# A two-layer decoder trunk: pairs' weights in their own buffer on GpSimd's queue, two gate halves split by transfers, and turned blocks placed first on ScalarE

## The chip, the cores and the metric

The kernel runs on one core of one Trainium2 chip. The time is the device time of one execution in microseconds (us); lower is better. A profiled execution is taken by the hardware profiler and shows, for each engine, when each instruction ran and what ended the idle time before it.

Engines, by the names of the profile: PE is TensorE's products, PEld its weight loads, DVE is VectorE, ACT is ScalarE, POOL is GpSimd, SP is SyncE, which here issues nearly all transfers. A DMA "lands" when its data is there and its semaphore says so. L12 is line 12 of the kernel before.

## What is computed

A trunk of two pre-norm residual layers over 256 tokens of width 1024, all in float32. Cut to what matters here:

```python
for i in range(2):
    u = rmsnorm(h, attn_norm_g[i])
    h = h + mixer_i(u) @ w_o[i]             # 16 heads of 64; layer 0 forgetting attention, layer 1 MoBA
    u = rmsnorm(h, ffn_norm_g[i])
    gu = u @ ffn_w_in[i]                    # 1024 x 5632
    h = h + (silu(gu[:, :2816]) * gu[:, 2816:]) @ ffn_w_out[i]     # 2816 x 1024
    gate = sigmoid(rmsnorm(h, ple_norm_g[i]) @ ple_w_gate[i])      # 1024 x 1024
    h = h + gate * (p[i] @ ple_w_up[i])     # p: 256 x 256
return rmsnorm(h, final_norm_g)
```

## The kernel before, in words

**Products of halves.** float32 operands are split into a rounded high half (type fp32r) and the low rest, `lo = x - hi`. A product is three products of halves: high by high, high by low, low by high (`mm3`, L94 to L98). So every block of weights is loaded by SyncE into a raw tile, rounded into `whi` by ScalarE and subtracted into `wlo` by VectorE: `half` (L129, the splits at L158 and L159), `blocks`, and `gapped` (L167, splits at L175 and L176), whose weights are padded to 1080 columns. `raw` has six buffers, `whi` and `wlo` six each. A `raw` buffer is free when VectorE has made the low half; a `whi` slot is free when TensorE has used it.

**Order.** The program is written once, in one order; a scheduler then fixes each engine's order, and each engine executes strictly in that order, waiting on semaphores. `tc.issue_after(ins)` puts the instructions written inside it behind `ins` on the engine of `ins`; it adds no wait between engines. `tc.keep_in_program_order` fixes the order of the products at the end.

**Norms.** `Norm` (L181) turns h by TensorE transposes (`turn`, L196, result in PSUM tile `tp`). For each of the eight blocks of 128 columns ScalarE writes the high half times the norm's gain (`g`, L192) and VectorE the low half (L193). `square` (L206) lets ScalarE sum squares, `root` (L213) makes the factor 1/rms with one GpSimd power (`col`, L220), which is applied later.

**Before the FFN.** At the end of `attention` h is finished, squared and scaled (`hn`), with GpSimd's powers `coln` (L581, L582). `ple_up` (L754) makes p @ ple_w_up: four PSUM banks (`pu`), each copied by ScalarE into `ut` (L763; the trace names the tile uh). Then `nf.turn` transposes hn and the eight turned blocks are made.

**The FFN** (`ffn`, L590). There are 22 column tiles f of 128. `up([f])` makes gate and up products (`gu`, 48 products of 256 columns per f); `up([0, 1])` does two tiles together. `gated` (L647) applies silu and the product into `a`. Two tiles f make a unit u, eleven units in all. A unit's down projection runs as a scheme of seven block products instead of eight (`product`, L628, tile `fo`): it needs sums of activation blocks (L665 to L667, then split into `ah` and `al` by `halves`, L671) and sums of weight blocks. `unit(u)` (L599) loads the unit's weights of ffn_w_out in two transfers of 512 KB into `ru` (L603, raw buffers), splits them (`p0`, `p3`), makes four sums in `xs` (L617, L619, L622; two buffers, `xs2[:, u % 2]`) and splits these (`p1`, `p2`; L596 ScalarE into `uh`, L597 VectorE into `ul`). From f = 4 on, `visit` puts 11 of the 21 products of a unit ahead of the even f and 10 ahead of the odd f, so that a unit's period is 21 products of 512 columns and 96 of 256 columns. The second product of high halves by `al` is the third of its visit. The last unit's split halves take `whi` and `wlo` slots.

**The gate.** After the last visits `gate` takes the first two halves of ple_w_gate with `half()`. `onto` adds the sums to h, `np_.turn(0)` transposes the first four blocks, `np_.square(0)` squares, and two more halves follow. `ple` (L765) makes the products `pg` (`pair_unit`, one half for two blocks k), in the middle `nm.turn(1)`, `nm.square(1)` and `nm.root()`.

Of the kernel before, what the change touches and what calls it, by code (L numbers as in the profile page):

```python
# [46 lines left out]
HW = 1024  # L47
HC = 512
NCHUNK = 54
WARM = 10  # L50
RAW = 6
# [3 lines left out]
LINE = 64  # L55
# [13 lines left out]
NU = FT // 2  # L69
# [6 lines left out]
def trunk(ctx: ExitStack, tc: tile.TileContext, x, xg, wx, xr, pt, w, wu, cst, gf, rel, hot, rvm, out):  # L76
    nc = tc.nc
# [49 lines left out]
    state = {"next": 0}  # L127

    def half(at=0, entry=0):  # L129


        i = state["next"]
        state["next"] += 1
        if i not in (1, 2):
            raw = work.tile([P, HW + LINE], F32, tag="raw", bufs=RAW, name=f"raw{i}")
        ht, lt = (work.tile([P, HW + 2 * LINE], F32R, tag=n, bufs=6, name=f"{n}{i}") for n in ("whi", "wlo"))
        hi, lo = ht[:, at:at + HW], lt[:, at:at + HW]
        if entry:
            nc.sync.dma_start(raw[:, 0:HW], w[i - 2][:, 0:HW])
            nc.scalar.activation(hi, raw[:, 0:HW], AF.Copy)  # L140
            ats = [(at + FURTHER, 0, entry), (at + LINE, entry, HW)]
            for a, c0, c1 in ats:
                nc.vector.tensor_tensor(lt[:, a + c0:a + c1], raw[:, c0:c1], f32(hi[:, c0:c1]), op=ALU.subtract)
            return hi, [lt[:, a + k * P:a + (k + 1) * P] for a, c0, c1 in ats for k in range(c0 // P, c1 // P)]
        if i in (1, 2):
            raw = hw[:, i - 1, S:]
        parts = 2 if i < 2 else 1
        for q in range(parts):
            c = slice(q * HW // parts, (q + 1) * HW // parts)
            if i in (1, 2):  # L150
                at = slice(c.start + (S if q else 0), c.stop + S)
                nc.sync.dma_start(hw[:, i - 1, at], wx[i - 1][:, at])
            else:
                nc.sync.dma_start(raw[:, c], w[max(i - 2, 0)][:, c])
            if i + q == 0:
                nc.vector.tensor_copy(hi[:, c], raw[:, c])
            else:
                nc.scalar.activation(hi[:, c], raw[:, c], AF.Copy)  # L158
            nc.vector.tensor_tensor(lo[:, c], raw[:, c], f32(hi[:, c]), op=ALU.subtract)  # L159
        return hi, lo  # L160
# [17 lines left out]
        return [[t[:, c:c + P] for c in cs] for t in (ht, lt)]  # L178


    class Norm:  # L181


# [5 lines left out]

        def block(self, m, src):  # L190
            g = gn[:, self.n, m:m + 1]
            nc.scalar.activation(self.hi[:, m], src, AF.Copy, scale=g)  # L192
            self.last = nc.vector.scalar_tensor_tensor(self.lo[:, m], src, g, f32(self.hi[:, m]),  # L193
                                                       op0=ALU.mult, op1=ALU.subtract)

        def turn(self, hf, src=h, keep=lambda i: i):  # L196

            for b in (2 * hf, 2 * hf + 1):
                tp = bank(f"tp{self.n}_{b}")
                for n in range(4):  # L200
                    m, t = 2 * b + n // 2, n % 2
                    keep(nc.tensor.transpose(tp[:, n * P:(n + 1) * P], src[:, t, m * P:(m + 1) * P], ident))
                for n in range(2):
                    self.block(2 * b + n, tp[:, n * S:(n + 1) * S])

        def square(self, hf):  # L206
            for t in range(2):
# [28 lines left out]
    nm = Norm(0)  # L236
# [31 lines left out]
    def tokens(o, x, t, w, start, stop):  # L268

        at = slice(t * P, (t + 1) * P)  # L270
        mm3(o, (x[0][:, at], x[1][:, at]), w, start, stop)
# [109 lines left out]
    def attention(layer, nm, mid, early, nf, fill):  # L381
# [191 lines left out]
        for t in range(2):  # L573
# [8 lines left out]
            nc.gpsimd.tensor_tensor(r, r, nhalf[:, 0:1], op=ALU.pow)  # L582
            nc.scalar.activation(hn[:, t, 0:HC], h[:, t, 0:HC], AF.Copy, scale=r)
            nc.vector.tensor_scalar(hn[:, t, HC:D], h[:, t, HC:D], r, None, op0=ALU.mult)
        ple_up(layer, pp, ut)
        for hf in range(2):
            nf.turn(hf, hn)
        return ut

    def ffn(layer, nm):  # L590
        xs2 = work.tile([P, 2, 4, HC], F32, tag="act", name=f"xs{layer}")
        np_ = Norm(3 * layer + 2)
        left, right = {}, {}

        def splits(hi, lo, src):
            nc.scalar.activation(hi, src, AF.Copy)  # L596
            return nc.vector.tensor_tensor(lo, src, f32(hi), op=ALU.subtract)  # L597

        def unit(u):  # L599

            r1, r2 = (work.tile([P, HW + LINE], F32, tag="raw", bufs=RAW, name=f"ru{layer}_{u}_{i}") for i in range(2))
            for i, r in enumerate((r1, r2)):
                nc.sync.dma_start(r[:, 0:HW], wu[layer * NU + u][:, i * HW:(i + 1) * HW])  # L603
            xs = xs2[:, u % 2]

            def pair(n, wide=HW):
                if u == NU - 1:
                    return [work.tile([P, HW + 2 * LINE], F32R, tag=t, bufs=6, name=f"{t}u{layer}_{n}")[:, 0:wide]
                            for t in ("whi", "wlo")]
                return [stage.tile([P, wide], F32R, tag=f"{t}{n}", bufs=1, name=f"{t}{n}_{layer}_{u}")  # L610
                        for t in ("uh", "ul")]

            p0 = pair(0)
            splits(*p0, r1[:, 0:HW])
            p3 = pair(3, HC)
            splits(*p3, r2[:, HC:HW])
            nc.vector.tensor_tensor(xs[:, 0:2], r2[:, 0:HC].unsqueeze(1).to_broadcast([P, 2, HC]),  # L617
                                    r1[:, 0:HW].rearrange("p (a c) -> p a c", c=HC), op=ALU.add)
            nc.vector.tensor_tensor(xs[:, 2], xs[:, 0], r1[:, HC:HW], op=ALU.add)  # L619
            p1 = pair(1)  # L620
            splits(*p1, xs[:, 0:2].rearrange("p a c -> p (a c)"))
            nc.vector.tensor_tensor(xs[:, 3], xs[:, 2], r2[:, HC:HW], op=ALU.add)  # L622
            p2 = pair(2)
            splits(*p2, xs[:, 2:4].rearrange("p a c -> p (a c)"))
            cut = lambda p, i: [t[:, i * HC:(i + 1) * HC] for t in p]
            right[u] = {1: cut(p0, 0), 3: cut(p0, 1), 2: p3, 5: cut(p1, 0), 7: cut(p1, 1), 6: cut(p2, 0), 4: cut(p2, 1)}
# [52 lines left out]
        def up(fs):  # L679

            bks = {f: bank(f"gu{layer}_{f}") for f in fs}

            def step(f, a, wt, k, start):
                mm3(bks[f][:, a * S:(a + 1) * S], (wt[0][k], wt[1][k]), nm.k(k), start, k == KT - 1)

            if fs[0] == 0:
                wts = {f: (blocks() if f else gapped(), blocks()) for f in fs}
                for k in range(KT):
                    for f in fs:
                        for a in range(2):  # L690
                            step(f, a, wts[f][a], k, k == 0 and a == 0)
            else:
                for a in range(2):
                    wt = blocks() if a else gapped()
                    for k in range(KT):
                        step(fs[0], a, wt, k, k == 0)
            for f in fs:
                gated(f, bks[f])

        up([0, 1])  # L700
        up([2])
        up([3])
        acc = {i: bank(f"fo{layer}_{i}") for i in (1, 3, 2, 5, 7, 6, 4)}
        for f in range(4, FT):
# [1 line left out]
            up([f])  # L706
        for u in (NU - 2, NU - 1):
            unit(u)
        gate = [half(), half()]
        def last(u, *which):  # L710
            for i in which:
                for n in range(3):
# [5 lines left out]

        last(NU - 2, 1, 2, 6, 7, 4)
        last(NU - 1, 1, 2, 6, 7, 4)  # L720
        with tc.issue_after(left["end"].ins):
            onto(0, 0, acc[1])
            onto(0, 0, acc[2])
        u2 = work.tile([P, HC], F32, tag="t2k", bufs=3, name=f"u2_{layer}")
# [9 lines left out]
        np_.turn(0, h, tc.keep_in_program_order)  # L734
        with tc.issue_after(got.ins):
            onto(0, 1, u2, ALU.subtract)
        with tc.issue_after(np_.last.ins):
            onto(1, 1, u3, ALU.subtract)
            onto(1, 1, acc[5])
            onto(0, 1, acc[5])  # L740
            got = onto(0, 1, acc[3])
        np_.square(0)
        with tc.issue_after(got.ins):
            gate += [half(), half()]
        return np_, gate

    def ple_in(layer):
# [6 lines left out]
    def ple_up(layer, pp, ut):  # L754
        phi, plo = pp
        wt = [half(), half()]
        for hf in range(2):
            cols = slice(hf * HC, (hf + 1) * HC)
            for t in range(2):
                bk = bank(f"pu{layer}_{hf}_{t}")  # L760
                for k in range(2):
                    tokens(bk, (phi[:, k], plo[:, k]), t, [w[:, cols] for w in wt[k]], k == 0, k == 1)
                nc.scalar.activation(ut[:, t, cols], bk, AF.Copy)  # L763

    def ple(layer, nm, ut, nx, early):  # L765

# [9 lines left out]
        for c in range(4):  # L776
            pair_unit(bks[0], c, early[c], nm.k, mid=(lambda: nm.turn(1)) if c == 1 else None)
            if c == 1:
                nm.square(1)
                nm.root()  # L780
                table(AF.Sigmoid, nm.col[:, 0:1])
        for t in range(2):
# [194 lines left out]
```

## Time and profile before

| | |
|---|---|
| runs, median (lowest to highest) | 657.89 us (656.99 to 659.89), three runs |
| profiled execution, its own time | 657.68 us |
| its span | 655.8 us |
| TensorE busy | 637.9 us (97%) |
| VectorE busy | 525.7 us (80%) |
| ScalarE busy | 422.7 us (64%) |
| GpSimd busy | 14.8 us (2%), 27 instructions |
| granted TensorE clock, mean | 0.997 |
| DMA, mean rate over the span | 191 GB/s |

The span is the time between the first and the last event of the program on the core; the execution's own time is 1.9 us longer. A row of the timeline has the start in us from the start of the span, the duration, the engine, the line, the instruction, the tile written and the tiles read, their shapes, the count, and in brackets the idle time before it and what ended that. Products are pipelined: TensorE starts the next one before the modelled end of the one before, so that the distance of two starts, not the duration, is the price of a product. A wait in the lists is "engine line waited for: us in total, times, longest us".

### The profile page before, as it was taken

How to read it: one execution, taken by the hardware profiler on the slowest of the kernel's cores; microseconds unless marked ns; L12 is line 12 of the kernel's file. 1: busy time of each engine (PE TensorE's matmuls, PEld its weight loads, DVE VectorE, ACT ScalarE, POOL GpSimd, SP SyncE). 2: the span in 40 equal slices, each digit the busy share in tenths (PEclk: the TensorE clock that was granted, in tenths of full speed). 3: DMA queues.
4: the chain of work that ended last, by engine and by line, in shares of the span. 5: the costliest groups of instructions: out<-in, count | busy, mean ns of one | idle time of the engine just before them, and what ended most of it. 6: DMA issues, size and time to landing. Idle time of an engine off the chain costs nothing.

```text
span 655.8 us, 11673 instructions
## 1 busy us (share of the span) xinstructions
PE 637.9 (97%) x4514; PEld 575.6 (88%) x4514; DVE 525.7 (80%) x828; ACT 422.7 (64%) x725; POOL 14.8 (2%) x27
## 2 busy tenths in 40 slices
PE   9999999999999999999999999999999999999995
PEld 7899987899989899997889999789999888989874
DVE  5878874799888888898875787659888888889985
ACT  6966674777655566557666677667766555555663
POOL 1000000100000000000200000010000000000001
PEclk9999999999999999999999999999999999999998
DMA  8969544467656666541797554444675665655501
GB/s 336 385 223 313 173 129 147 147 196 263 196 198 196 195 198 196 194 146 51 245 356 222 180 170 132 132 130 152 222 235 179 196 195 194 199 195 171 183 1 64
DMA packets 36022, 125.20 MB, mean 191 GB/s; under 512 B 3904, under 2 KB 6272, under 8 KB 35968
## 3 DMA queue, kind: packets, MB, share of 16 engines
q1 hardware_dynamic: 35552, 124.07, 57.6%
q8 instruction: 35, 0.57, 0.4%
q10 hardware_dynamic: 416, 0.40, 0.2%
q14 instruction: 19, 0.16, 0.1%
HBM read 123.39 MB, written 4.22 MB: 195 GB/s over the span
## 4 chain that ended last, share of the span: by engine, by line
PE 62%; DVE 16%; DMA 10%; issue 6%; ACT 4%; POOL 1%; POOLq 0%; DVEq 0%; ACTq 0%
DMA ru<-wu 9%; PE fo L632 7%; PE gu L97 6%; PE gu L98 6%; PE gu L96 6%; DVE wlo L176 5%; PE pq L96 5%; PE pq L97 4%; PE pq L98 4%; DVE wlo L159 4%; PE wo L96 2%; PE v L97 2%; PE v L98 2%; PE wo L97 2%; PE wo L98 2%
## 5 line engine op out<-in xcount | busy, mean ns | idle before, releaser
L96 PE MATMUL gu<-g,whi 128*128 128x256 f32 x704 | 194.0, 277 | 1.9 <-ACT g L192 1.9
L97 PE MATMUL gu<-g,whi 128*128 128x256 f32 x704 | 194.6, 277 | 0.5 <-DVE g L193 0.5
L98 PE MATMUL gu<-g,wlo 128*128 128x256 f32 x704 | 194.5, 277 | 0.0
L158 ACT ACTIVATE whi<-raw 128x1024 fp32r<-128x1024 f32 (+1 forms) x122 | 128.3, 1057 | 94.9 <-PE gu L97 51.4
L159 DVE TENSOR_TENSOR wlo<-raw,whi 128x1024 fp32r<-128x1024 f32 (+1 forms) x123 | 147.7, 1211 | 28.0 <-ACT whi L158 27.8
L96 PEld LDWEIGHTS gu<-g,whi 128*128 128x128 f32 x704 | 131.8, 188 | 3.8 <-ACT g L192 2.3
L97 PEld LDWEIGHTS gu<-g,whi 128*128 128x128 f32 x704 | 132.2, 188 | 2.4 <-DVE g L193 0.9
L98 PEld LDWEIGHTS gu<-g,wlo 128*128 128x128 f32 x704 | 132.1, 188 | 0.0
L175 ACT ACTIVATE whi<-raw 128x1080 fp32r<-128x1080 f32 x47 | 52.2, 1112 | 57.9 <-PE gu L97 40.2
L176 DVE TENSOR_TENSOR wlo<-raw,whi 128x1080 fp32r<-128x1080 f32 x47 | 60.0, 1277 | 18.4 <-ACT whi L175 18.3
L96 PE MATMUL pq<-g,whi 128*128 128x256 f32 x256 | 71.5, 279 | 0.0
L97 PE MATMUL pq<-g,whi 128*128 128x256 f32 x256 | 70.9, 277 | 0.0
L98 PE MATMUL pq<-g,wlo 128*128 128x256 f32 x256 | 70.9, 277 | 0.0
L632 PE MATMUL fo<-uh,al 128*128 128x512 f32 x140 | 56.3, 402 | 4.9 <-DVE al L597 4.8
L617 DVE TENSOR_TENSOR xs<-ru,ru 128x1024 f32<-128x1024 f32 x22 | 26.9, 1223 | 38.0 <-DMA ru<-wu 38.0
L632 PE MATMUL fo<-uh,ah 128*128 128x512 f32 x140 | 55.0, 393 | 0.0
L632 PE MATMUL fo<-ul,ah 128*128 128x512 f32 x140 | 54.8, 392 | 0.0
L96 PEld LDWEIGHTS pq<-g,whi 128*128 128x128 f32 x256 | 48.2, 188 | 1.1 <-issue 0.6
L597 DVE TENSOR_TENSOR ul<-xs,uh 128x1024 fp32r<-128x1024 f32 x40 | 48.7, 1217 | 0.0
L97 PEld LDWEIGHTS pq<-g,whi 128*128 128x128 f32 x256 | 48.1, 188 | 0.0
L98 PEld LDWEIGHTS pq<-g,wlo 128*128 128x128 f32 x256 | 48.1, 188 | 0.0
L596 ACT ACTIVATE uh<-xs 128x1024 fp32r<-128x1024 f32 x40 | 40.3, 1057 | 6.3 <-DVE xs L617 5.6
(189 smaller groups left out, 1129.6 us busy)
## 6 DMA issues: line engine op xcount, KB each, us to landing
raw<-w SPq DMA_DIRECT2D x122, 512.0 KB, 4.5
raw<-w SPq DMA_DIRECT2D x47, 540.0 KB, 4.5
ru<-wu SPq DMA_DIRECT2D x44, 512.0 KB, 4.0
d<-d SPq DMA_DIRECT2D x4, 768.0 KB, 9.8
bias<-d SPq DMA_DIRECT2D x4, 512.0 KB, 5.2
h<-x SPq DMA_DIRECT2D x2, 512.0 KB, 9.2
hw<-wx SPq DMA_DIRECT2D x1, 640.0 KB, 6.4
hw<-xr SPq DMA_DIRECT2D x1, 640.0 KB, 8.3
```

The lines of the kernel that those rows point to most:

```text
L96: mm(o, ah, bh, start=start, stop=False, skip_group_check=True)
L97: mm(o, ah, bl, start=False, stop=False, skip_group_check=True)
L98: mm(o, al, bh, start=False, stop=stop, skip_group_check=True)
L158: nc.scalar.activation(hi[:, c], raw[:, c], AF.Copy)
L159: nc.vector.tensor_tensor(lo[:, c], raw[:, c], f32(hi[:, c]), op=ALU.subtract)
L175: nc.scalar.activation(ht, raw[:, 0:WW], AF.Copy)
L176: nc.vector.tensor_tensor(lt, raw[:, 0:WW], f32(ht), op=ALU.subtract)
L596: nc.scalar.activation(hi, src, AF.Copy)
L597: return nc.vector.tensor_tensor(lo, src, f32(hi), op=ALU.subtract)
L617: nc.vector.tensor_tensor(xs[:, 0:2], r2[:, 0:HC].unsqueeze(1).to_broadcast([P, 2, HC]), r1[:, 0:HW].rearrange("p (a c) -> p a c", c=HC), ...
L632: got = mm(acc[i], a[x][:, SLOT[i]], b[y], start=u == 0 and n == 0, stop=u == NU - 1 and n == 2, skip_group_check=True)
```

## The change

It has three parts.

*Pairs' weights.* The "act" buffer that held two sets of sums now holds one set (`xs`) and the two halves of a unit's raw weights (`ru1`, `ru2`). Units 0 to 9 load these through GpSimd's queue; the last unit still uses two raw buffers and SyncE. The halves `p3` get a second buffer and leave the `whi` and `wlo` slots in the last unit.

*First gate halves.* `summed()` takes the place of `half()` for the first two halves of ple_w_gate: a transfer on GpSimd's queue writes the weight into hi, of type fp32r, and so rounds it; ScalarE writes -hi into lo; a second transfer adds the weight to lo. The negations stand behind the last rounding of the activations on ScalarE.

*Turned blocks.* `ple_up` first issues all products, with a bank for each, and returns the copies to be issued by its caller: three before the turned blocks, the fourth after them. `behind()` puts instructions behind the last turned block on ScalarE and on VectorE; it is used for the splits of `up([2])`, for both squares of the gate's norm, for VectorE's last sums onto h and for gate halves 2 and 3.

```diff
+    def summed():
+        i = state["next"]
+        state["next"] += 1
+        hi, lo = (work.tile([P, HW + 2 * LINE], F32R, tag=n, bufs=6, name=f"{n}{i}")[:, 0:HW] for n in ("whi", "wlo"))
+        nc.gpsimd.dma_start(hi, w[i - 2][:, 0:HW])
+        nc.scalar.activation(lo, f32(hi), AF.Copy, scale=-1.0)
+        nc.gpsimd.dma_start(lo, w[i - 2][:, 0:HW], accum_op=ALU.add)
+        return hi, lo
...
+        def behind(self):
+            both = ExitStack()
+            for i in (self.first, self.last):
+                both.enter_context(tc.issue_after(i.ins))
+            return both
...
-        ple_up(layer, pp, ut)
+        empty = ple_up(layer, pp, ut)
+        for n in range(3):
+            empty(n)
         for hf in range(2):
             nf.turn(hf, hn)
+        with nf.behind():
+            empty(3)
...
-        xs2 = work.tile([P, 2, 4, HC], F32, tag="act", name=f"xs{layer}")
+        xr8 = work.tile([P, 8, HC], F32, tag="act", name=f"xr{layer}")
+        xs, ru1, ru2 = (xr8[:, i:j] for i, j in ((0, 4), (4, 6), (6, 8)))
...
-            r1, r2 = (work.tile([P, HW + LINE], F32, tag="raw", bufs=RAW, name=f"ru{layer}_{u}_{i}") for i in range(2))
+            r1, r2, queue = ru1, ru2, nc.gpsimd
+            if u == NU - 1:
+                r1, r2 = (work.tile([P, HW + LINE], F32, tag="raw", bufs=RAW, name=f"ru{layer}_{i}")[:, 0:HW]
+                          for i in range(2))
+                queue = nc.sync
             for i, r in enumerate((r1, r2)):
-                nc.sync.dma_start(r[:, 0:HW], wu[layer * NU + u][:, i * HW:(i + 1) * HW])
-            xs = xs2[:, u % 2]
+                queue.dma_start(r, wu[layer * NU + u][:, i * HW:(i + 1) * HW])
             def pair(n, wide=HW):
-                if u == NU - 1:
+                if u == NU - 1 and n != 3:
...
-                return [stage.tile([P, wide], F32R, tag=f"{t}{n}", bufs=1, name=f"{t}{n}_{layer}_{u}")
+                return [stage.tile([P, wide], F32R, tag=f"{t}{n}", bufs=1 + (n == 3), name=f"{t}{n}_{layer}_{u}")
...
-        up([2])
+        with nm.behind():
+            up([2])
...
-        gate = [half(), half()]
+        rounded, split = left["end"]
+        with tc.issue_after(rounded.ins):
+            gate = [summed(), summed()]
...
-        with tc.issue_after(np_.last.ins):
+        with np_.behind():
             onto(1, 1, u3, ALU.subtract)
             onto(1, 1, acc[5])
             onto(0, 1, acc[5])
             got = onto(0, 1, acc[3])
-        np_.square(0)
-        with tc.issue_after(got.ins):
-            gate += [half(), half()]
+            np_.square(0)
+            with tc.issue_after(got.ins):
+                gate += [half(), half()]
...
+        bks = [bank(f"pu{layer}_{n}") for n in range(4)]
...
+        for n in range(4):
+            for k in range(2):
+                tokens(bks[n], (phi[:, k], plo[:, k]), n % 2, [w[:, at(n)] for w in wt[k]], k == 0, k == 1)
+        return lambda n: nc.scalar.activation(ut[:, n % 2, at(n)], bks[n], AF.Copy)
...
             if c == 1:
-                nm.square(1)
+                with nm.behind():
+                    nm.square(1)
                 nm.root()
```

More of the change, by code (lines that the diff above doesn't have):

```diff
@@ L191, in block @@
             g = gn[:, self.n, m:m + 1]
-            nc.scalar.activation(self.hi[:, m], src, AF.Copy, scale=g)
+            self.first = nc.scalar.activation(self.hi[:, m], src, AF.Copy, scale=g)
             self.last = nc.vector.scalar_tensor_tensor(self.lo[:, m], src, g, f32(self.hi[:, m]),
@@ L584, in attention @@
             nc.vector.tensor_scalar(hn[:, t, HC:D], h[:, t, HC:D], r, None, op0=ALU.mult)
-        ple_up(layer, pp, ut)
+        empty = ple_up(layer, pp, ut)
+        for n in range(3):
+            empty(n)
         for hf in range(2):
             nf.turn(hf, hn)
+        with nf.behind():
+            empty(3)
         return ut
     def ffn(layer, nm):
-        xs2 = work.tile([P, 2, 4, HC], F32, tag="act", name=f"xs{layer}")
+        xr8 = work.tile([P, 8, HC], F32, tag="act", name=f"xr{layer}")
+        xs, ru1, ru2 = (xr8[:, i:j] for i, j in ((0, 4), (4, 6), (6, 8)))
+        ru1, ru2 = (r.rearrange("p a c -> p (a c)") for r in (ru1, ru2))
         np_ = Norm(3 * layer + 2)
@@ L595, in splits @@
         def splits(hi, lo, src):
-            nc.scalar.activation(hi, src, AF.Copy)
-            return nc.vector.tensor_tensor(lo, src, f32(hi), op=ALU.subtract)
+            first = nc.scalar.activation(hi, src, AF.Copy)
+            return first, nc.vector.tensor_tensor(lo, src, f32(hi), op=ALU.subtract)
         def unit(u):
-            r1, r2 = (work.tile([P, HW + LINE], F32, tag="raw", bufs=RAW, name=f"ru{layer}_{u}_{i}") for i in range(2))
+            r1, r2, queue = ru1, ru2, nc.gpsimd
[3 more added lines that the diff above has]
+                queue = nc.sync
             for i, r in enumerate((r1, r2)):
-                nc.sync.dma_start(r[:, 0:HW], wu[layer * NU + u][:, i * HW:(i + 1) * HW])
-            xs = xs2[:, u % 2]
+                queue.dma_start(r, wu[layer * NU + u][:, i * HW:(i + 1) * HW])
             def pair(n, wide=HW):
-                if u == NU - 1:
+                if u == NU - 1 and n != 3:
                     return [work.tile([P, HW + 2 * LINE], F32R, tag=t, bufs=6, name=f"{t}u{layer}_{n}")[:, 0:wide]
                             for t in ("whi", "wlo")]
-                return [stage.tile([P, wide], F32R, tag=f"{t}{n}", bufs=1, name=f"{t}{n}_{layer}_{u}")
+                return [stage.tile([P, wide], F32R, tag=f"{t}{n}", bufs=1 + (n == 3), name=f"{t}{n}_{layer}_{u}")
                         for t in ("uh", "ul")]
@@ L720, in ffn @@
         last(NU - 1, 1, 2, 6, 7, 4)
-        with tc.issue_after(left["end"].ins):
+        with tc.issue_after(split.ins):
             onto(0, 0, acc[1])
@@ L756, in ple_up, with at @@
         wt = [half(), half()]
[L757 to L763, printed above, removed]
+        bks = [bank(f"pu{layer}_{n}") for n in range(4)]
+        def at(n):
+            return slice(n // 2 * HC, (n // 2 + 1) * HC)
+        for n in range(4):
+            for k in range(2):
+                tokens(bks[n], (phi[:, k], plo[:, k]), n % 2, [w[:, at(n)] for w in wt[k]], k == 0, k == 1)
+        return lambda n: nc.scalar.activation(ut[:, n % 2, at(n)], bks[n], AF.Copy)
     def ple(layer, nm, ut, nx, early):
```

## The prediction

> **What bounds the kernel now.** I read the page's busy line and the list of TensorE's own waits first. TensorE is busy 637.9 of 655.8 us, so a change can only win the time in which TensorE is held up, and that list names the places.
>
> ```profile
> core 0 of [0], span 655.8 us
> PE 637.9 (97%) x4514; PEld 575.6 (88%) x4514; DVE 525.7 (80%) x828; ACT 422.7 (64%) x725; POOL 14.8 (2%) x27
> ...
> PE fo L632 <- DVE al L597: 4.8, 11, 0.9
> PE gu L96 <- ACT g L192: 1.9, 2, 0.9
> PE pg L96 <- ACT g L192: 0.9, 2, 0.5
> ```
>
> The columns are total us, times, longest. First the down products (fo) wait for VectorE's low half of the activations (al); then the first gate/up products (gu) and the gate products (pg) wait for ScalarE's turned blocks (g).
>
> The first figure understates its loss, because a stalled product's modelled end hides part of the gap. The starts of the down products in TensorE's timeline give it whole; these rows open the part-0 visits of units 0, 1 and 9 in layer 0, then of units 0 and 9 in layer 1.
>
> ```profile
> 146.49 0.40 PE L632 MATMUL fo<-uh,ah 128*128 128x512 f32 x1
> 162.24 0.40 PE L632 MATMUL fo<-uh,ah 128*128 128x512 f32 x1
> 291.88 0.40 PE L632 MATMUL fo<-uh,ah 128*128 128x512 f32 x1
> 466.11 0.40 PE L632 MATMUL fo<-uh,ah 128*128 128x512 f32 x1
> 613.01 0.40 PE L632 MATMUL fo<-uh,ah 128*128 128x512 f32 x1
> ```
>
> An undisturbed unit lasts 162.24 - 146.49 = 15.75 us, nine of them 141.75. Layer 0 takes 291.88 - 146.49 = 145.39 and layer 1 takes 613.01 - 466.11 = 146.90. The down projections thus lose 3.64 + 5.15 = 8.8 us.
>
> Why al is late stands in VectorE's timeline of one unit, TensorE's answer and SyncE's list of waits:
>
> ```profile
> 221.87 1.23 DVE L617 TENSOR_TENSOR xs<-ru,ru 128x1024 f32<-128x1024 f32 x1 [2.90 <-DMA ru<-wu]
> ...
> 226.67 1.08 DVE L597 TENSOR_TENSOR al<-a,ah 128x896 fp32r<-128x896 f32 x1
> ...
> 229.15 1.22 DVE L597 TENSOR_TENSOR ul<-xs,uh 128x1024 fp32r<-128x1024 f32 x1
> 227.81 0.50 PE L632 MATMUL fo<-uh,al 128*128 128x512 f32 x1 [0.62 <-DVE al L597]
> SPq L603 <- DVE wlo L176: 75.9, 18, 5.6
> ```
>
> VectorE runs in order. It sits 2.90 us at the sum xs until the pair's weights (ru) have landed; al comes behind it with four instructions between. ru lands late because SyncE may issue it only when an earlier weight has left one of the six raw buffers (75.9 us waiting at L603).
>
> **A, the pairs' buffers.** Ten of a layer's eleven units now load into their own ru1 and ru2 through GpSimd's queue: 40 of the 44 transfers at L603 leave SyncE, and raw serves w alone. The sums xs, two buffers before, now have one: xs of unit u+1 may be written only after the second ul of unit u has read it (the row at 229.15), which follows al. So al no longer stands behind a sum that waits for a transfer; 2.90 us come off VectorE's path against a TensorE gap of 0.62 here and 0.9 at most. What is late next? ul of the pair, which TensorE needs as the eleventh product; it too moves up. The new wait is GpSimd's: the next ru may be issued only when all readers are through, the last being
>
> ```profile
> 217.76 0.68 DVE L597 TENSOR_TENSOR ul<-ru,uh 128x512 fp32r<-128x512 f32 x1
> ```
>
> and the next sum is due at 229.15 + 1.22 = 230.4 in today's order, at worst 2.9 earlier. That leaves 9.0 to 11.9 us after 217.76 + 0.68 = 218.4 for the two transfers; GpSimd has no other work inside a down projection, so nothing queues behind. I take 90% of 8.8, a gain of 7.9, since the first and last units have other orders (the last stays on SyncE). Bounds: a loss (rival S) to 8.8.
>
> In front of unit 0 the loads go past GpSimd's norm steps (coln). If both issues stand ahead of them and cost one GpSimd step each (0.70, row below), 1.4 us per layer lie before the transposes; the up-projection of p (pu) covers part of that. I take 0, as the slot that ru needs is free only when the output projection ends, and the scheduler may put ru behind.
>
> **B, turned blocks first.** Start of layer 0's FFN, TensorE, then ScalarE, then VectorE:
>
> ```profile
> 121.19 1.91 PE L202 MATMUL tp<-con,uh 128*128 128x128 f32 x16
> 124.02 0.62 PE L96 MATMUL gu<-g,whi 128*128 128x256 f32 x3 [0.92 <-ACT g L192]
> 124.88 0.39 PE L97 MATMUL gu<-g,whi 128*128 128x256 f32 x1 [0.24 <-DVE g L193]
> 120.57 1.55 ACT L763 ACTIVATE uh<-pu 128x512 f32<-128x512 f32 x3
> 122.00 1.11 ACT L175 ACTIVATE whi<-raw 128x1080 fp32r<-128x1080 f32 x1
> 122.99 0.60 ACT L763 ACTIVATE uh<-pu 128x512 f32<-128x512 f32 x1
> 123.47 0.86 ACT L192 ACTIVATE g<-tp,gx 128x256 fp32r<-128x256 f32 x2
> 123.14 1.28 DVE L176 TENSOR_TENSOR wlo<-raw,whi 128x1080 fp32r<-128x1080 f32 x1 [2.72 <-ACT whi L175]
> ```
>
> The change puts the fourth uh and the split of up([2]) (whi at 122.00, wlo at 123.14) behind all eight blocks. g then starts when the third uh ends, near 122.1, not 123.47: 1.35 earlier against a wait of 0.92, and wlo no longer holds VectorE's g, which removes the 0.24. That gains (0.92 + 0.24) x 2 layers = 2.3; bounds 1.2 (one of the causes stays) to 3.1 (the hidden part counted as in A, 8.8 against 4.8 seen, which is more than I trust). What moves back costs nothing: the split is needed only after the 96 products of up([0, 1]), which are the larger part of a 15.75 us unit, and it moves by about 3.
>
> **C, the gate's norm.** ScalarE now squares h after the turned blocks. Before, one square stood between:
>
> ```profile
> 309.90 0.62 ACT L209 ACTIVATE sq<-h 128x512 f32<-128x512 f32 x1
> 308.90 2.35 DVE L159 TENSOR_TENSOR wlo<-raw,whi 128x1024 fp32r<-128x1024 f32 x2
> ```
>
> Taking it away covers the 0.9 us of the pg row above; I take all 0.9, bounds 0 and 1.3. The two squares end later by about their own length, and with them the norm's root; the second column half of products covers that. The splits of gate halves 2 and 3 also move behind the blocks; VectorE got to them only at 308.90 anyway.
>
> **D, the first two gate halves.** Per layer two SyncE loads, two ScalarE roundings and two VectorE subtractions go; four GpSimd transfers and two ScalarE negations come. VectorE's two subtractions, 2.35 us by the row above, are off the path: TensorE's waits name no wlo. New is a chain: ScalarE negates hi, held behind the last rounding of the activations, then the transfer adds the weight. Landing must precede the second product of each half:
>
> ```profile
> 291.97 1.06 ACT L158 ACTIVATE whi<-raw 128x1024 fp32r<-128x1024 f32 x1 [1.66 <-PE gu L97]
> 296.11 0.63 ACT L596 ACTIVATE ah<-a 128x512 fp32r<-128x512 f32 x1 [0.93 <-DVE a L667]
> 303.49 0.40 PE L97 MATMUL pg<-wlo,g 128*128 128x512 f32 x1
> 306.25 0.39 PE L97 MATMUL pg<-wlo,g 128*128 128x512 f32 x1
> raw<-w SPq DMA_DIRECT2D x8, 512.0 KB, 4.3
> ```
>
> The rounding ends at 296.74; two negations at the 1.06 us of a rounding of this size (first row) end at 297.8 and 298.9. Until 303.49 there are 5.7 us, until 306.25 there are 7.4. A plain load of this size takes 4.3 from issue to landing in this stage (the last row, window 280 to 312). No row shows a transfer that rounds or adds. Bounds: 4.3 (no cost; perhaps 0.3 gained from a freer VectorE) and the slowest 512 KB load of the page:
>
> ```profile
> h<-x SPq DMA_DIRECT2D x2, 512.0 KB, 9.2
> ```
>
> I take about 6, nearer to the first row, since the queue is nearly empty by then: 0.3 late per layer, 0.6 in all. Behind a waiting negation on ScalarE stands the copy u2, on which the transposes hang; its hi is there before, as the last whi slot needed comes free by 291.97 and 291.97 + 4.3 = 296.3. [...]
>
> **The sum.** 7.9 + 2.3 + 0.9 - 0.6 = 10.5 us off the profiled execution's own 657.68 us gives 647.2. That execution lies 0.2 below the median of the three runs, 657.89, so nothing is corrected.
>
> **Rivals.** *S, the single buffer starves (slower).* If the two ru transfers take longer than their cover, VectorE waits at xs in every unit and holds all that follows. VectorE works without a break from 221.87 to 235.34 + 0.29 = 235.63, 13.8 us; of 15.75 that leaves 2.0, so it decides from 9.0 + 2.0 = 11 us. Each us beyond costs about 16 us in some 16 units. What speaks for it is that GpSimd is held up by VectorE:
>
> ```profile
> 314.28 3.81 POOL L220 TENSOR_TENSOR col<-ms,nhalf 128x2 f32<-128x2 f32 x1 [194.38 <-DVE ms L218]
> 335.15 0.70 POOL L220 TENSOR_TENSOR col<-ms,nhalf 128x2 f32<-128x2 f32 x1 [17.06 <-DVE ms L218]
> 314.04 3.49 DVE L159 TENSOR_TENSOR wlo<-raw,whi 128x1024 fp32r<-128x1024 f32 x3
> 235.34 0.29 DVE L667 TENSOR_TENSOR a<-a 128x128 f32<-128x128 f32 x1
> 199.68 5.44 DMA ru<-wu
> ```
>
> The same step takes 3.1 us more beside three subtractions. If each issue of ru were held so, the pair would need the 5.4 us that the chain of waits shows for ru + 6.2 = 11.6, just past the point. At 12 us: 657.7 + 16 - 8.8 - 2.3 - 0.9 + 0.6 = 662.3. [...] Chance 0.10.
>
> *L, the adding transfers are late.* At 9.2 us each the first low half lands 3.5 late, the second with it: 7.4 for both layers in place of 0.6, hence 654.0. For it: no row. Against: the nearly empty queue. Chance 0.15.
>
> *O, the change does not do what it says.* The instruction order follows the scheduler's estimates; if another waiting instruction lands ahead of al, only a third of A comes, 2.9: 657.7 - 2.9 - 2.3 - 0.9 + 0.6 = 652.2. Chance 0.13.
>
> **How the numbers follow.** The forecast has 0.62, with a spread of its own from 644 (all upper bounds) to 651 (B and C small). L and O lie inside a range of 644.0 to 655.5; S is left out. Half a per cent, about what a measurement of this kernel can tell from no change, is 3.3 us: faster means under 654.6. Forecast 0.60, O 0.10 and L 0.08 make 0.78; S makes slower 0.10; the rest, 0.12, is the same.
>
> **What would show it.** Right: units of 15.75 us throughout, no row of fo waiting for al, no xs waiting for ru longer than VectorE's slack; the first gu within 0.2 us of the last transpose; pg's second product at once. Wrong: VectorE waiting at xs with ru in flight on GpSimd's queue (S), pg waiting for wlo from a transfer (L), fo still waiting for al with something else ahead of it (O), or GpSimd's coln later than ScalarE's square by more than 0.5 us.

## The result and the profile after

The changed kernel takes 649.41 us (median of four runs, 648.65 to 651.09) against 658.1 us for the kernel before on the same chip (656.99 to 659.89): ratio 0.9869, 95% interval 0.9839 to 0.9899. Its profiled execution took 649.11 us, where the forecast was 647.2; its span is 647.3.

The page's busy line, after:

```profile
PE 636.0 (98%) x4514; PEld 578.6 (89%) x4514; DVE 522.3 (81%) x824; ACT 420.6 (65%) x725; POOL 41.1 (6%) x75
```

TensorE's list of waits, after (us in total, times, longest):

```profile
PE pg L97 <- DMA wlo<-w: 1.3, 1, 1.3
PE cold L115 <- PEq L1001: 0.8, 1, 0.8
PE po L525 <- ACT pt L516: 0.5, 2, 0.3
PE fo L658 <- DVE al L620: 0.5, 2, 0.3
```

The eleven waits for al are two, and the waits for turned blocks (gu and pg, from g) are gone. A new one has come: pg waits for a low half written by a transfer. TensorE's timeline at the first down products of units 0, 1 and 9 in layer 0 and of units 0 and 9 in layer 1:

```profile
145.22 0.39 PE L658 MATMUL fo<-uh,ah 128*128 128x512 f32 x1
161.48 0.40 PE L658 MATMUL fo<-uh,ah 128*128 128x512 f32 x1
287.46 0.40 PE L658 MATMUL fo<-uh,ah 128*128 128x512 f32 x1
460.37 0.40 PE L658 MATMUL fo<-uh,ah 128*128 128x512 f32 x1
602.67 0.40 PE L658 MATMUL fo<-uh,ah 128*128 128x512 f32 x1
```

Unit 0 takes 16.26 us and the other eight (287.46 - 161.48) / 8 = 15.75 each: all but the first are undisturbed. Unit 0 is late because unit 1's transfers can start only when unit 0's sums have emptied the one buffer. The timelines of GpSimd, VectorE and TensorE:

```profile
132.67 0.54 POOL L630 DMA_DIRECT2D xr<-wu  x1 [11.32 <-DVE xr L645]
134.40 0.54 POOL L630 DMA_DIRECT2D xr<-wu  x1 [1.20 <-ACT whi L175]
139.91 1.22 DVE L643 TENSOR_TENSOR xr<-xr 128x1024 f32<-128x1024 f32 x1 [2.15 <-DMA xr<-wu]
144.91 1.08 DVE L620 TENSOR_TENSOR al<-a,ah 128x896 fp32r<-128x896 f32 x1
146.06 0.50 PE L658 MATMUL fo<-uh,al 128*128 128x512 f32 x1 [0.21 <-DVE al L620]
```

The first transfer waits for a sum (L645); the second is issued at 134.40, 0.5 us behind the end of the last sum, and the profile puts its wait down to a rounding on ScalarE that came later still. VectorE stands 2.15 us at unit 1's sum until the pair has landed, and unit 0's al is queued behind it. At the other end, the gate of layer 1 (ScalarE, GpSimd, TensorE):

```profile
607.69 1.99 ACT L187 ACTIVATE wlo<-whi 128x1024 fp32r<-128x1024 f32 x2
609.03 1.80 POOL L188 DMA_DIRECT2D wlo<-w  x2 [8.21 <-ACT wlo L187]
619.31 0.50 PE L97 MATMUL pg<-wlo,g 128*128 128x512 f32 x1 [1.30 <-DMA wlo<-w]
```

The second adding transfer is issued half-way through the 1.80 us, near 609.9, and lands near 619.3: 9.3 us. The list of issues gives the medians, after (KB each, us from issue to landing):

```profile
wlo<-w POOLq DMA_DIRECT2D x4, 512.0 KB, 6.4
whi<-w POOLq DMA_DIRECT2D x4, 512.0 KB, 3.7
xr<-wu POOLq DMA_DIRECT2D x40, 512.0 KB, 5.9
```

An addition takes 6.4, a transfer that only rounds 3.7, a pair's 5.9.

Cut at TensorE's product starts, the profiled executions divide as follows (us). "To unit 0" is the span's start to the first down product, "units" the nine periods from unit 0 to unit 9, "tail 0" unit 9 of layer 0 to the first v of layer 1, "v to unit 0" from there to layer 1's first down product, "tail 1" unit 9 of layer 1 to the span's end. A row is one execution. Three lie over 2.5 us from the median of their runs: e2 and e3 above it, e11 below.

| run | to unit 0 | units, layer 0 | tail 0 | v to unit 0 | units, layer 1 | tail 1 | span |
|---|---|---|---|---|---|---|---|
| before | 146.49 | 145.39 | 36.10 | 138.13 | 146.90 | 42.79 | 655.8 |
| after | 145.22 | 142.24 | 35.74 | 137.17 | 142.30 | 44.63 | 647.3 |
| e1 one half ahead | 145.82 | 143.02 | 35.60 | 140.64 | 141.72 | 42.80 | 649.6 |
| e2 no transfers | 147.22 | 142.29 | 37.63 | 138.73 | 144.10 | 44.73 | 654.7 |
| e3 buffers only | 148.82 | 146.30 | 38.39 | 137.87 | 145.29 | 45.53 | 662.2 |
| e4 blocks only | 146.43 | 149.76 | 36.10 | 137.86 | 147.81 | 42.74 | 660.7 |
| e5 first unit raw | 147.11 | 149.79 | 35.75 | 137.54 | 149.49 | 42.92 | 662.6 |
| e6 e1 and e5 | 146.33 | 147.96 | 35.59 | 137.51 | 149.65 | 42.76 | 659.8 |
| e7 buffers only, first raw | 146.56 | 150.46 | 38.38 | 138.69 | 149.70 | 45.31 | 669.1 |
| e8 own buffer by SyncE | 145.23 | 141.72 | 36.04 | 136.47 | 141.72 | 43.52 | 644.7 |
| e9 e8 and one half ahead | 145.45 | 141.72 | 35.61 | 136.07 | 141.72 | 42.53 | 643.1 |
| e10 e2, last sums apart | 145.46 | 142.27 | 34.80 | 137.98 | 142.28 | 41.91 | 644.7 |
| e11 raw by GpSimd | 146.50 | 148.62 | 36.08 | 137.92 | 151.17 | 43.01 | 663.3 |
| e12 pairs twice | 145.40 | 186.79 | 36.06 | 136.84 | 190.42 | 46.29 | 741.8 |

Of the 8.50 us between before and after, 3.15 + 4.60 = 7.75 come from the units, 1.27 and 0.96 from the stretches ahead of them, 0.36 from tail 0; tail 1 gives 1.84 back.

### The profile page after: what moved, and what is told of

Its sections match the earlier page's. It is cut to its first block, busy times and chain, and to the rows that moved or that the text cites. A ratio compares the mean times of both kernels' runs of the same rounds, so it can differ in the third digit from the quotient of the medians.

```text
span 647.3 us, 11656 instructions
## 1 busy us (share of the span) xinstructions
PE 636.0 (98%) x4514; PEld 578.6 (89%) x4514; DVE 522.3 (81%) x824; ACT 420.6 (65%) x725; POOL 41.1 (6%) x75
## 4 chain that ended last, share of the span: by engine, by line
PE 87%; DMA 4%; issue 3%; DVE 2%; ACT 1%; POOL 1%; POOLq 0%; ACTq 0%; DVEq 0%
PE fo L658 15%; PE gu L97 11%; PE gu L96 10%; PE gu L98 10%; PE pq L96 5%; PE pq L97 5%; PE pq L98 5%; DMA xr<-wu 3%; PE wo L96 2%; PE wo L98 2%; PE wo L97 2%; PE v L98 2%; PE v L96 2%; PE v L97 2%; PE pg L96 2%
## 5 line engine op out<-in xcount | busy, mean ns | idle before, releaser
L159 DVE TENSOR_TENSOR wlo<-raw,whi 128x1024 fp32r<-128x1024 f32 (+1 forms) x119 | 143.6, 1213 | 45.1 <-ACT whi L158 43.4
L158 ACT ACTIVATE whi<-raw 128x1024 fp32r<-128x1024 f32 (+1 forms) x118 | 122.9, 1055 | 79.4 <-PE gu L97 37.2
L620 DVE TENSOR_TENSOR ul<-xr,uh 128x1024 fp32r<-128x1024 f32 (+1 forms) x80 | 85.8, 1088 | 1.9 <-ACT uh L619 1.9
L619 ACT ACTIVATE uh<-xr 128x1024 fp32r<-128x1024 f32 (+1 forms) x80 | 73.4, 953 | 10.6 <-DMA xr<-wu 9.1
L630 POOL DMA_DIRECT2D xr<-wu x40 | 21.7, 543 | 263.5 <-DVE ul L620 195.3
```

Source lines behind the costliest of these rows:

```text
L619: first = nc.scalar.activation(hi, src, AF.Copy)
L620: return first, nc.vector.tensor_tensor(lo, src, f32(hi), op=ALU.subtract)
L630: queue.dma_start(r, wu[layer * NU + u][:, i * HW:(i + 1) * HW])
```

## The experiments

**e1: the first half by transfers issued ahead.** The negations and adding transfers stood behind the last rounding; here the first pair of them is issued in the last unit, before its sums' splits.

```diff
-        left, right = {}, {}
+        left, right, gate = {}, {}, []
...
-            splits(*p3, r2[:, HC:HW])
+            splits(*p3, r2[:, HC:HW]); gate.extend([summed()] if u == NU - 1 else [])
...
         with tc.issue_after(rounded.ins):
-            gate = [summed(), summed()]
+            gate.append(summed())
```

> The first of the two gate halves is split earlier: its rounding transfer, ScalarE's negation and the adding transfer stand before the last unit's p1, so that only the second adding transfer starts behind the last rounding of the activations. Theory (the adding transfers of the changed kernel land late in layer 1 because two start together and share the queue with another load): TensorE's wait of 1.3 us for wlo goes, and 0.3 us of the late copy u2 per layer; 1.5 to 2.5 us below the changed kernel, near 647.3. Rival (the gate's loss comes from ScalarE's order and the late transposes, not from the transfers): the wait for wlo goes but the first gate product starts as late as before, at most 0.7 us gained, 648.7.

651.17 us against 660.4 on that chip, ratio 0.985 (0.9822 to 0.9878); the interval overlaps the changed kernel's, so the time does not tell the two apart. TensorE no longer waits for wlo of the gate, and tail 1 is 42.80, 1.83 less than in the changed kernel. The tail's loss was the late transfer. The profile lost elsewhere, most of it ahead of layer 1's first unit (VectorE, then TensorE):

```profile
458.24 1.23 DVE L643 TENSOR_TENSOR xr<-xr 128x1024 f32<-128x1024 f32 x1 [5.05 <-DMA xr<-wu]
460.86 0.38 PE L98 MATMUL gu<-g,wlo 128*128 128x256 f32 x1 [2.67 <-DVE wlo L159]
```

This is the first fill again: unit 1's pair goes into a buffer that unit 0 has only just emptied. The second transfer of this fill took 5.4 to 7.6 us from issue to landing in the ten layers of after, e1, e2, e3 and e10, and what VectorE has queued behind the sum (wlo of up, then al) pays for it.

**e2: no transfers for the gate.** The two halves are split on the engines.

```diff
-        with tc.issue_after(rounded.ins):
-            gate = [summed(), summed()]
+        if True:
+            gate = [half(), half()]
```

> Only the first two gate halves are undone: they are loaded by SyncE, rounded by ScalarE and subtracted by VectorE again; the rest of the change stays. Theory (the transfers' late landing is the loss, VectorE has time): 1.5 to 2 us below the changed kernel, near 647.6. Rival (the two subtractions now stand ahead of the last low halves of the activations on VectorE, which sits right before TensorE's last down products): TensorE waits 1 to 2 us per layer for al at the end of the down projection, and the time is equal to or up to 2 us above the changed kernel, 649.4 to 651.4.

653.78 us, ratio 0.9886 (0.9856 to 0.9915). The theory did not come, and the rival had the place but not the tile: TensorE waits in the last unit, for ah and not for al. Tail 0 is 37.63, worse than after and worse than before. The timelines of VectorE (the last unit's first sum), ScalarE and TensorE:

```profile
287.15 1.22 DVE L643 TENSOR_TENSOR xr<-ru,ru 128x1024 f32<-128x1024 f32 x1
291.34 2.01 ACT L158 ACTIVATE whi<-raw 128x1024 fp32r<-128x1024 f32 x2
293.24 0.52 ACT L619 ACTIVATE ah<-a 128x384 fp32r<-128x384 f32 x1
293.81 0.50 PE L658 MATMUL fo<-whiu,ah 128*128 128x512 f32 x1 [0.71 <-ACT ah L619]
296.72 0.50 PE L658 MATMUL fo<-whiu,ah 128*128 128x512 f32 x1 [1.01 <-ACT ah L619]
```

The last unit's ah is late, behind two roundings of the gate. In the kernel before these roundings hurt nobody, so something else had moved them together (e10).

**e3: the pairs' buffers alone**, the kernel before with only the first part of the change.

```diff
-        xs2 = work.tile([P, 2, 4, HC], F32, tag="act", name=f"xs{layer}")
+        xr8 = work.tile([P, 8, HC], F32, tag="act", name=f"xr{layer}")
+        xs, ru1, ru2 = (xr8[:, i:j] for i, j in ((0, 4), (4, 6), (6, 8)))
...
+            r1, r2, queue = ru1, ru2, nc.gpsimd
```

> The kernel before with the pairs' own buffers on GpSimd's queue alone. Theory (the parts add up): units of 15.75 us, 7.7 us gained as in the changed kernel, near 650.4 us. Rival (the own buffers need the earlier turned blocks or the freer VectorE of the other parts): less than 6 us, above 652.

657.63 us, ratio 0.9971 (0.9947 to 0.9995): nearly nothing. In the profiled execution units 1 to 8 take 15.75 in both layers, but unit 0 takes 20.3 and 19.3, and both tails are 2.3 to 2.7 longer than before. TensorE's waits:

```profile
PE fo L637 <- ACT ah L598: 4.7, 5, 1.3
PE fo L637 <- DVE al L599: 3.2, 2, 1.6
```

VectorE's first fill:

```profile
141.68 1.23 DVE L622 TENSOR_TENSOR xr<-xr 128x1024 f32<-128x1024 f32 x1 [4.25 <-DMA xr<-wu]
```

The sum now stands even ahead of a's products, so a, ah and al all come after the landing. The profiled execution is the slowest of the ten (663.96 us). That the first unit's loss is what differs between the ten is likely, but only one of them has a trace.

**e4: the turned blocks alone**, the kernel before with `ple_up` and `up([2])` of the third part, without the edits of the gate's norm.

```diff
+        with nf.behind():
+            empty(3)
...
-        up([2])
+        with nm.behind():
+            up([2])
```

> The kernel before with the turned blocks ahead of the fourth copy and of the third tile's split alone; pairs and gate as before. Theory: TensorE's wait for g at the start of each FFN goes, 2.4 us gained, near 655.7 us. Rival (what is won at the start of the FFN is lost again in the first units of the down projection, whose splits come later): under 1 us, above 657.

663.58 us, ratio 1.004 (1.0018 to 1.0062): slower. The scheduler filled the freed place between the blocks with the pair's splits, which in this kernel are ready (ScalarE and VectorE, e4), but in the changed kernel come after seven blocks (ScalarE, after):

```profile
122.08 1.06 ACT L607 ACTIVATE uh<-ru 128x1024 fp32r<-128x1024 f32 x1
122.77 1.23 DVE L628 TENSOR_TENSOR xs<-ru,ru 128x1024 f32<-128x1024 f32 x1 [2.27 <-DMA ru<-wu]
```

```profile
122.18 2.67 ACT L202 ACTIVATE g<-tp,gx 128x256 fp32r<-128x256 f32 x7
124.73 1.07 ACT L619 ACTIVATE uh<-xr 128x1024 fp32r<-128x1024 f32 x1
```

Counted from the output projection's last product, TensorE's first gate/up product starts 0.5 us earlier than before in each layer (1.2 in the changed kernel), and next to nothing of that is left at the first down product (146.43 and 137.86 in the table against 146.49 and 138.13). So the third part's gain at the start depends on the first part, and the units wait more for al, 9.7 us in 12 waits (149.76 and 147.81).

**e5, e6, e7: unit 0 by raw buffers.** If the first fill is the trouble, unit 0's pairs can take raw buffers, as in the kernel before, so that the own buffer stands empty for unit 1.

```diff
-            if u == NU - 1:
+            if u in (0, NU - 1):
```

On the changed kernel (e5):

> The changed kernel, except that unit 0 loads its pairs as before (two raw buffers, SyncE), so that the pairs' own buffer stands empty when unit 1's transfers are issued. Theory (first fill): with one buffer, unit 1's transfers wait for unit 0's last sums (issued at 132.7 and 134.4 us in the changed kernel), land 5 to 8 us later, and the sum that waits for them stands in VectorE's queue ahead of low halves that TensorE needs; here the wait of VectorE for the pairs' transfer (2.2 and 2.4 us in the changed kernel, up to 5.1 in the other runs) and the late al of unit 0 (period 16.3 instead of 15.75 us) are gone: 1.0 us less than the changed kernel by its profile, more where its first landing was late; 646 to 649 us, ratio to before 0.981 to 0.987. Rival (SyncE's raw buffers are the scarce ones at the stage's start): two raw buffers held by unit 0 make gate and up weights late, TensorE waits for whi or wlo there, and it is level with the changed kernel or up to 2 us slower.

On e1 (e6):

> Both amendments: the first of the two halves by transfers is issued ahead, and unit 0's pairs go to raw buffers. If the two waits are separate, the gains add up: no wait for wlo of the gate at the end, none for wlo at the stage's start: 1.3 us less than with the raw buffers alone, 645 to 648 us, ratio 0.980 to 0.985. Rival: what the one gives is taken by the other (the first transfer of the gate on GpSimd's queue stands ahead of pairs' transfers, or the tail is bound by VectorE anyway), and it is level with the better of the two.

On e3 (e7):

> The pairs' buffers alone, without the other two parts, with unit 0's pairs in raw buffers. Theory (first fill): the buffers alone gained only 0.3% because at the start of each FFN VectorE waited 4.2 and 2.4 us for the refilled buffer, al came late, TensorE waited 1.3 and 1.6 us and its granted clock then fell to 0.50 for some 7 us; without that the nine units take 142 us in both layers instead of 146.3 and 145.3, and the ratio falls from 0.997 to 0.984 to 0.989; the waits of 0.7 and 1.0 us for ah in the last unit of each layer, for which the gate's roundings on ScalarE are to blame, remain. Rival (order): it is the turned blocks' order, not the first fill, that the buffers need; then the first unit is late again (over 18 us) and the ratio stays above 0.994.

All three were slower than the kernel before (656.7 us on that chip): e5 664.38 us, ratio 1.0112 (1.008 to 1.0145); e6 662.49, 1.0089 (1.0073 to 1.0106); e7 668.75, 1.0187 (1.0147 to 1.0227). Unit 0 was cured as expected: 15.74 or 15.75 in all six layers. But most units behind it took 16 to 18.5, one in e7 19.9. ScalarE's and TensorE's waits in e5:

```profile
ACT uh L619 <- DMA xr<-wu: 59.3, 11, 7.0
PE gu L96 <- ACT sg L677: 11.3, 13, 2.4
```

In the changed kernel ScalarE waits 9.1 us for pairs, 1.9 at most. In e5 ScalarE stands at the split of most later pairs before they have landed, with the next gate/up work behind it. The fill theory was right on unit 0 and its remedy wrong: the edit shifted the order of all units. Why the scheduler then chose that order was not settled.

**e8: the own buffer filled by SyncE.**

```diff
-            r1, r2, queue = ru1, ru2, nc.gpsimd
+            r1, r2, queue = ru1, ru2, nc.sync
```

> The changed kernel with the pairs' own buffers filled by SyncE's queue in place of GpSimd's. Theory: the buffer frees the raw buffers, but SyncE executes in order, so a pair's transfer that waits for its buffer holds up the raw loads written behind it; each unit's period is then between the 15.75 us of the changed kernel and the 16.4 of before: 650 to 656 us. Rival: the buffer alone is what counts, SyncE is never held up for long, and it is within 1 us of the changed kernel (648 to 650), or faster, since a transfer by SyncE lands in 4.5 us at the median against 5.9.

646.93 us, ratio 0.985 (0.9832 to 0.9868). My theory fell: SyncE was not held up to any harm, and all eighteen units take 15.75, unit 0 among them, since the scheduler here puts unit 1's sum behind unit 0's al (VectorE):

```profile
142.91 1.09 DVE L620 TENSOR_TENSOR al<-a,ah 128x896 fp32r<-128x896 f32 x1
147.18 1.22 DVE L643 TENSOR_TENSOR xr<-xr 128x1024 f32<-128x1024 f32 x1
```

The landing is not shorter:

```profile
xr<-wu SPq DMA_DIRECT2D x40, 512.0 KB, 6.0
```

6.0 us against GpSimd's 5.9. The buffer counts, not the queue. (Every run with the buffer also has the second buffer of the halves p3, which was not tried alone.)

**e9: e8 and the first half ahead.** Both edits together.

> The changed kernel with the pairs' own buffers filled by SyncE and with the first of the two gate halves by transfers issued ahead. If both gains are separate: the run by SyncE had no late first unit (period 15.75 from the first unit on) but still 0.6 us of waiting for wlo of the gate and 35.8 us from the last unit to the last product; the run with the half ahead had 34.7 there. So 1 to 1.5 us less than by SyncE alone: 645 to 646 us on a chip with 657 before, ratio 0.981 to 0.985. Rival (the half ahead is noise): level with SyncE alone, ratio 0.985.

645.23 us (644.88 to 645.42), against 656.02 before: ratio 0.9831 (0.9804 to 0.9857). That is where the theory had it, but the interval includes the rival's 0.985; what speaks for the theory is the profile, whose tails are 0.43 and 0.99 us shorter than in e8. The span is 643.1, 4.2 under the changed kernel's, and TensorE waits neither for al nor for wlo. This version has the lowest ratio of all; its interval still overlaps that of the changed kernel.

**e10: e2 with the last unit's sums apart.** The change keeps one set of sums where there were two. In the last unit the own buffer is free (its pair is in raw), so its sums can go there.

```diff
+            x4 = xr8[:, 4:8] if u == NU - 1 else xs
...
-            nc.vector.tensor_tensor(xs[:, 2], xs[:, 0], r1[:, HC:HW], op=ALU.add)
+            nc.vector.tensor_tensor(x4[:, 2], x4[:, 0], r1[:, HC:HW], op=ALU.add)
...
```

> The run without the transfers by addition (both gate halves split on the engines), except that the last unit's sums are written to the pairs' own buffer, which is free by then, and not to xs. Theory (single xs): the change takes away the second set of sums, so the last unit's sums wait for the splits of the unit before, come some 4 us late, and the rounding of gate halves then collides with ah: the waits for ah of 0.7 and 1.0 us per layer. With the sums apart these waits are gone; the way from the last unit to the next layer's first product falls from 37.6 to 36.0 us, and in the second layer likewise: 3 us less than without this edit, ratio to before 0.982 to 0.986 where it was 0.9886. Rival (the gate halves by themselves make ah late, since a unit is 0.7 us shorter): the waits stay, ratio 0.987 to 0.990.

647.29 us (645.12 to 650.18), ratio 0.9866 (0.9825 to 0.9906), an interval that holds theory and rival alike. The waits decide: those for ah are gone, and the tails are the shortest of all, 34.80 and 41.91: 2.8 us per layer less than e2. The cause of the late ah was the single set of sums; with it mended, and the gate halves split on the engines, the tails are 0.9 and 2.7 us shorter than the changed kernel's. The first fill is still there (TensorE waits 1.6 us for wlo behind it); whether the spread of the four runs comes from it is not shown. This edit with SyncE's queue was not run.

**e11: only the queue**, raw buffers as before.

```diff
-                nc.sync.dma_start(r[:, 0:HW], wu[layer * NU + u][:, i * HW:(i + 1) * HW])
+                nc.gpsimd.dma_start(r[:, 0:HW], wu[layer * NU + u][:, i * HW:(i + 1) * HW])
```

> The kernel before, with nothing changed but the queue: units' weights go to the raw buffers as before, by GpSimd's queue. Theory (the buffer counts, not the queue): al stays late in most units, since a raw buffer still comes free only in turn; units of 16.2 to 16.9 us, ratio 0.99 to 1.01. Rival (the queue counts: SyncE's order delayed the units' weights): units near 15.75 and a ratio of 0.988 or less.

671.67 us, ratio 1.0248 (1.0213 to 1.0283), worse than the theory's bound of 1.01. Units still take up to 17.5 us, and TensorE still waits for al, 11.3 us in 14 waits. With e8 this separates the two: the buffer gains, the queue alone loses.

**e12: every pair transferred twice.**

```diff
-                queue.dma_start(r, wu[layer * NU + u][:, i * HW:(i + 1) * HW])
+                for _ in range(1 + (u < NU - 1)):
+                    queue.dma_start(r, wu[layer * NU + u][:, i * HW:(i + 1) * HW])
```

> The changed kernel with each transfer of a pair by GpSimd's queue made twice (units 0 to 9 of both layers), into the same place. It doubles the time to landing and tells how much cover the single buffer has. The prediction put the point at 11 us for a pair, from which each us costs about 16. By the theory that the cover holds to 11 us: a pair that lands in 9 to 11 us costs under 4 us beyond the changed kernel (649 to 653), one of 12 us or more 10 to 20 us (659 to 669). Rival: the cover is far shorter, since ScalarE takes the pair first and stands ahead of the next up weights (its waits for the pair were up to 1.9 us in the changed kernel): then every us of landing over 6 counts, and 11 us cost 40 or more (690).

742.44 us, ratio 1.1313 (1.1262 to 1.1363), far above the theory's 669 at most; the rival had 690 or more. The second transfer into a place waits for the first: in the unit before, GpSimd waits 4.18 and 0.72 us for the landings ahead of its third and fourth issue (at 219.90 and 221.15). One unit, from GpSimd's first issue over ScalarE to TensorE:

```profile
235.66 0.54 POOL L631 DMA_DIRECT2D xr<-wu  x1 [13.97 <-DVE ul L620]
250.40 0.63 ACT L619 ACTIVATE uh<-xr 128x512 fp32r<-128x512 f32 x1 [7.13 <-DMA xr<-wu]
253.56 0.58 PE L96 MATMUL gu<-g,whi 128*128 128x256 f32 x1 [4.28 <-ACT sg L678]
```

The window around the wait's end (busy times of PE, PEld, DVE, ACT and POOL, then the granted clock, DMA share and GB/s):

```profile
253.00:257.00 4.00, 3.44 (x16) 3.44 (x17) 4.00 (x5) 1.45 (x3) 0.00 (x0) 0.57 0.45 122
```

ScalarE stands at the pair's split, and the copies out of PSUM (sg) that TensorE needs come behind it: the place that the rival named. The pair is used 14.74 us after its first issue and TensorE waits 4.28, so without cost it could have taken 10.5; the unit before gives 11.5 (14.23 less 2.71). Forecast: 11. But each us past it costs more than itself, and the clock reads 0.57 here. The eighteen units are 5.2 us longer than 15.75 on average, of which waits are 3.3 (59.4 us in all). The granted clock over the units is 0.91 in both layers; an estimate from this, 0.09 of 377.2 us, is 1.9 us per unit, the rest.

## Why the prediction was right, step by step

**A held in its size and in its reason for a running unit, and missed the ends.** Forecast 7.9, measured 7.75 in the units. The step "al no longer stands behind a sum that waits for a transfer" held for units 1 to 9; for unit 0 it did not (0.51 and 0.58 us in the profile, 4.6 in e3). The cover of 9.0 to 11.9 us was worked out for a running unit, and the first refill has no such cover. The raw buffers, which the prediction named as the reason for the late pairs, were the reason; the queue was no part of the gain (e8, e11). And the step on the single xs asked only what follows within a unit. The prediction did not ask what it does to the last unit, whose sums now wait for the splits of the unit before. By e2 and e10 that costs 2.8 us per layer when the gate halves are split on the engines.

**The loads past coln, taken at 0,** held: coln goes first, and the first pair's transfer is issued behind it at 120.05. By the order of the rows in e4 it was even useful: the pair's splits then come too late to stand between most of the blocks.

**B held,** as part of the whole: 2.37 (1.46 in layer 0 and 0.91 in layer 1, counted from the last attention products) against 2.3. TensorE's first gate/up product starts 7.34 and 7.33 us after the output projection's last, where it was 8.50 and 8.52: 1.16 and 1.19 less, and the prediction had 0.92 + 0.24 = 1.16 per layer. Alone, B gained nothing (e4).

**C held** as far as the waits show: the 0.9 of pg for g are gone.

**D is the term that was mis-sized.** It was put at -0.6 with a landing of 6 us. The median was 6.4, but one of the four took 9.3, as late as rival L had it. In e1 issuing one half ahead gives back 1.83 in layer 1 (0.14 in layer 0), in e9 against e8 0.99 (0.43). The prediction reckoned the first half as the tight one, but it was the second that came late: issued 0.95 us behind the first, it took 7.0 and 9.3 us, and 7.2 and 8.5 in e8, where the first took 5.4 to 5.9 and each of the eight that e1 and e9 issue apart 5.3 to 5.7. So the adding transfer issued right behind another landed late in both layers of both runs; why it is worse in layer 1 is not settled. Against the kernel before, tails 0 and 1 together changed by 0.36 - 1.84 = -1.5 where C and D were to give +0.3: 1.8 less, and the sum missed by 8.50 against 10.5.

**A term for the last unit was missing.** The three runs that differ in the gate halves and the sums divide the -1.5 further. Without transfers and with the sums apart (e10) the tails are 1.30 + 0.88 = 2.2 us shorter than before. The single set of sums then takes 2.83 + 2.82 = 5.7 (e2), and the transfers, which spare ScalarE the roundings that collide with ah, give 1.89 + 0.10 = 2.0 back. The prediction had neither the 5.7 nor the 2.0. That the profiled execution still came within 2 us of the forecast is in part luck.

**Side figures.** Three figures of the prediction do not come out of their own working: L at 3.5 late per layer makes 7.0 and 653.6, not 7.4 and 654.0; B's 2.3 scaled as 8.8 to 4.8 is 4.2, not the upper bound of 3.1; and with B and C at nothing the sum is 650.4, not 651. None of them stands in the sum.

**The rivals.** S, whose chance of 0.10 was the author's own estimate, did not come: TensorE waited in no unit but the first. A starved buffer does cost what S feared: e12 puts the point at 10.5 to 11.5 us, where the prediction had 11, and its price higher. But S had VectorE waiting at xs; in e12 it is ScalarE at the pair's split, so that the two points agree is luck. The hold-up that S feared for GpSimd's issues was not seen: in the changed kernel the forty take 0.54 us each on average (21.7 in all, the longest 0.75). The one at 134.40 lies wholly beside a subtraction of VectorE (134.34 to 135.62) and takes 0.54 too. The landing took 5.9 us by GpSimd and 6.0 by SyncE into the same buffer (e8). SyncE's queue cured unit 0 by the order of the instructions, not by a faster landing. L came once in four transfers. O came in part, at unit 0.

## What to carry to other kernels

When a double buffer is given up to pay for another, look at its last use and its first, not only at the running middle: here the middle gained 7.75 us, and in e3's profiled execution the first unit and the ends took more than that back. Parts of a change that share an in-order engine did not add up here (e3 and e4 alone give -0.3% and +0.4%, together with the gate's norm -1.1%, e2), so a forecast from parts needs each part's place in the other's order. Before a transfer is moved to another queue for a buffer's sake, try the buffer with the old queue.

## What the hardware showed unasked

After some of its short waits TensorE ran at a lower granted clock. In e3 TensorE waited 1.27 and 1.61 us shortly after each other; in e1 2.67 at once. The windows of e3, then of e1, then of e2 (the clock is third from the end):

```profile
148.00:150.00 2.00, 0.73 (x2) 0.30 (x2) 2.00 (x2) 2.00 (x3) 0.00 (x0) 0.99 0.86 280
150.00:157.00 7.00, 5.83 (x19) 4.96 (x20) 6.82 (x12) 2.31 (x4) 0.72 (x2) 0.52 0.85 288
157.00:160.00 3.00, 3.00 (x29) 3.00 (x28) 1.12 (x3) 1.11 (x1) 0.36 (x1) 1.00 0.88 259
```

```profile
461.00:462.00 1.00, 1.00 (x7) 1.00 (x8) 1.00 (x2) 0.96 (x2) 0.00 (x0) 0.67 0.26 49
462.00:464.00 2.00, 2.00 (x11) 2.00 (x11) 2.00 (x3) 2.00 (x3) 0.00 (x0) 0.50 0.64 234
464.00:465.00 1.00, 1.00 (x8) 1.00 (x7) 1.00 (x2) 1.00 (x2) 0.00 (x0) 0.62 0.68 206
```

```profile
462.00:464.00 2.00, 0.75 (x6) 0.75 (x7) 2.00 (x4) 0.57 (x1) 0.00 (x0) 1.00 0.00 0
464.00:468.00 4.00, 3.72 (x25) 3.11 (x25) 4.00 (x5) 4.00 (x6) 0.00 (x0) 1.00 0.71 235
```

In e3 the granted clock then read 0.52 over 7 us, in e1 0.67, 0.50 and 0.62 over 1, 2 and 1 us; in e2 a wait of 2.35 us, which ended at 463.25, left it at 1.00. Why waits of like length were followed by a lower clock in one run and not in another was not settled.

An adding transfer of 512 KB took 6.4 us at the median, 9.3 at worst, one that only rounds 3.7. Issued apart, as in e1 and e9, an adding transfer took 5.3 to 5.7.
